# Feed-forwards as block products in Strassen's form, with the sums on GpSimd

## The chip, the cores and the metric

The kernel runs on one core of one Trainium2 chip. Its time is device microseconds (us) of one execution. TensorE (PE in the profile) multiplies, its weight loads have a row of their own (PEld); VectorE (DVE), ScalarE (ACT) and GpSimd (POOL) do the elementwise work; SyncE (SP) issues the transfers. Each engine works through its own queue in order, and queues wait for one another by semaphores.

## The reference

Two layers over 512 tokens of 1024 features, all in float32. Each layer has a feed-forward, a mixer and a second feed-forward, each behind an RMS norm and added to x:

```
swiglu(h) = (silu(h @ w_gate) * (h @ w_up)) @ w_down          # 1024 -> 2816 -> 1024
x = x + 0.5 * swiglu(rmsnorm(x))
x = x + mixer(rmsnorm(x))      # layer 0: short convolution and attention over a memory
                               # layer 1: attention with forget gates, and over the memory
x = x + 0.5 * swiglu(rmsnorm(x))
```

The keys and values of layer 1's attention come from x as it enters that layer, under a norm of its own. A last norm ends it. So there are four feed-forwards, and the change is to them.

## The kernel before

Features lie on the 128 partitions, tokens along the free dimension: x is eight tiles `X[k]` of 128 x 512. Every product of a float32 weight block by a tile is three matmuls (`mm3`, lines 134 to 136): weight and tile are each split in a high and a low float32r part, and high x high, high x low and low x high are added in one PSUM bank of 512 columns. `Normed` splits x times the norm's gain; 1 / rms (`st.row`) is applied behind the product.

`Weights` holds the weights as pieces of up to 1024 columns in the order of use. `load` brings a piece to a raw tile (`wr`, four of them); `begin` splits it: ScalarE copies the high part (`wh`, line 81), VectorE subtracts it from the raw tile (`wl`, line 82), both of them SBUF. `next` hands a piece out and keeps the splits two pieces ahead of TensorE, the loads three.

`ffn` takes the 22 tiles of hidden features in two halves of 11. For a hidden tile TensorE multiplies a gate piece and an up piece by the eight tiles of x (48 matmuls). VectorE scales the gate from PSUM by 1 / rms (L287), ScalarE takes SiLU (L288), VectorE multiplies by the up product (L289), and the result is split (L139, L140). Then eight tiles of the down product take the half's 11 hidden tiles each; L308 scales the bank and L311 adds it to x. GpSimd has no work in a feed-forward. The order on each engine is the program's.

The first 57 us project the memory's keys (matmuls of 256 columns) and values; there, and in the last norm, some sums are on GpSimd (L159, L479, L792).

Of the kernel before, what the change touches and what calls it, by code (L numbers as in the profile page):

```python
# [22 lines left out]
HALVES = [(0, 11), (11, 22)]  # L23
# [12 lines left out]
class Weights:  # L36
    """Pieces of the weights in the order of use: loaded ahead, and split ahead into two float32r
    parts."""

    LOAD, SPLIT = 3, 2  # L40

    def __init__(self, nc, pool):
        self.nc, self.pool = nc, pool
        self.todo, self.raw, self.parts = [], {}, {}
        self.loaded = self.split = self.used = 0

    def add(self, ap, widths=(1024, 1024), step=1024):
        at = 0
        for w in widths:
            self.todo.append((ap[:, at : at + w], step))  # L50
            at += w
        assert at == ap.shape[1]

    def load(self):
        """The next piece, by transfers of step columns."""
        n = self.loaded
        self.loaded += 1
        ap, step = self.todo[n]
        w = ap.shape[1]
        self.raw[n] = self.pool.tile([P, 1024], F32, tag="wr", name=f"wr{n}", bufs=4)  # L60
        for a in range(0, w, step):
            c = slice(a, min(a + step, w))
            self.nc.sync.dma_start(out=self.raw[n][:, c], in_=ap[:, c])
            yield

    def begin(self):
        """The next piece's parts, split by step columns."""
        i = self.split
        self.split += 1
        while self.loaded < min(len(self.todo), i + 1 + self.LOAD):  # L70
            for _ in self.load():
                pass
        ap, step = self.todo[i]
        w, raw = ap.shape[1], self.raw.pop(i)
        hi = self.pool.tile([P, 1024], F32R, tag="wh", name=f"wh{i}", bufs=3)
        lo = self.pool.tile([P, 1024], F32R, tag="wl", name=f"wl{i}", bufs=3)
# [10 lines left out]
    def next(self, ahead=SPLIT):  # L87
        """The next piece's parts; the splits run ahead of it by so many pieces."""
        i = self.used
        self.used += 1  # L90
        while self.split < min(len(self.todo), i + 1 + ahead):
            for _ in self.begin():
                pass
        return self.parts.pop(i)
# [3 lines left out]
def model(ctx: ExitStack, tc: tile.TileContext, A, out):  # L98
# [13 lines left out]
    SLOTS = {"s": 66, "t": 12}  # L112
# [4 lines left out]
    def parts(tag="s"):  # L117
        return slot(tag, F32R), slot(tag, F32R)

# [12 lines left out]
    def mm3(ps, wh, wl, xh, xl, first, last):  # L132
        """One product over 128 rows: high x high, high x low, low x high."""
        nc.tensor.matmul(ps, wh, xh, start=first, stop=False)  # L134
        nc.tensor.matmul(ps, wh, xl, start=False, stop=False)  # L135
        nc.tensor.matmul(ps, wl, xh, start=False, stop=last)  # L136
# [10 lines left out]
    class Stats:  # L147
        """The squares of tiles of 128 features, summed; then 1 / rms by token."""
# [13 lines left out]
        def step1(self, c=None):  # L162
            """The sums over all features, on every partition, and their roots."""
# [14 lines left out]
        def columns(self):  # L178
            """1 / rms of the tokens of each block, by partition."""
# [10 lines left out]
    class Normed:  # L190
        """Tiles of x times a norm's gain, in two parts; 1 / rms is applied behind the product."""
# [14 lines left out]
    def plan_ffn(n):  # L206
        for a, b in HALVES:
            chunks(A["gu"][n, a:b])
            for d in range(KD):
                W.add(A["dn"][n, d][:, a * P : b * P], (6 * P, 5 * P))  # L210
# [17 lines left out]
    plan_ffn(3)  # L228

# [11 lines left out]
    # The tensor engine's clock rises while it works: it does from the first transfers on.  # L241
# [660 lines left out]
```

## Time and profile before

| | |
|---|---|
| time, median of 3 runs | 2038.25 us (2036.89 to 2038.62) |
| the profiled execution, its span | 2038.5 us |
| TensorE busy | 2018.4 us, 99% |
| VectorE busy | 1002.9 us, 49% |
| ScalarE busy | 704.7 us, 35% |
| GpSimd busy | 34.1 us, 2% |
| mean granted TensorE clock | 0.996 |
| HBM | 95 GB/s over the span |

Times in the rows are from the start of the span; the execution's own time is its span, 2038.5 us, a quarter of a microsecond over the median of the runs. A row of a timeline reads: start in us, duration in us, engine, line, operation, written tile <- read tiles, shapes, how many in a row, and in brackets how long the engine sat idle before it and what ended that. A row of a group has busy time and mean duration (ns) after the bar, then the idle time before the group's instructions and what ended it. Durations of matmuls overlap, since they are pipelined: their cost is read from the distance of their starts. `mm` and `aux` are PSUM banks; `s`, `t`, `r`, `wr`, `wh`, `wl` lie in SBUF.

### The profile page before, as it was taken

The page shows a single profiled execution, that of the slowest core. Times are in us where ns is not written, and L with a number is a line of the kernel's source. Part 1 is how long each engine was busy: PE and PEld are TensorE (multiplying, and loading weights), DVE is VectorE, ACT ScalarE, POOL GpSimd, SP SyncE. Part 2 cuts the span into 40 slices and gives each one's busy share as a digit, 9 for nine tenths or more (in the row PEclk, how much of TensorE's full clock was granted, in tenths as well). Part 3 has the DMA queues.
Part 4 walks back from the last instruction along what each step waited for, and adds up shares of the span by engine and source line. Part 5 has one row for each costly group of instructions (what it writes and reads, how often), then busy time and mean ns, then how long its engine had stood idle before and what let it go on. Part 6 is the DMA issues. An engine that isn't in the chain of part 4 may idle for free.

```text
span 2038.5 us, 22628 instructions
## 1 busy us (share of the span) xinstructions
PE 2018.4 (99%) x9175; PEld 1674.7 (82%) x9175; DVE 1002.9 (49%) x1355; ACT 704.7 (35%) x1049; POOL 34.1 (2%) x50
## 2 busy tenths in 40 slices
PE   9999999999999999999999999999999999999997
PEld 8788888888888888888888888888878878888886
DVE  7643434576555443443644343467546664344444
ACT  7422222353224332232432222335335552222233
POOL 2000000000000000000000000000001100000000
PEclk9999999999999999999999999999999999999998
DMA  7322332332222323322322332232221032233222
GB/s 261 105 94 79 117 99 82 99 104 73 98 99 93 100 84 91 118 94 76 120 94 86 91 114 98 80 112 77 80 93 63 32 103 94 84 102 106 98 78 70
DMA packets 62328, 195.73 MB, mean 96 GB/s; under 512 B 7056, under 2 KB 9232, under 8 KB 62224
## 3 DMA queue, kind: packets, MB, share of 16 engines
q1 hardware_dynamic: 62224, 194.30, 30.0%
q8 instruction: 71, 1.16, 0.2%
q14 instruction: 33, 0.27, 0.0%
HBM read 192.17 MB, written 2.10 MB: 95 GB/s over the span
## 4 chain that ended last, share of the span: by engine, by line
PE 98%; DVE 1%; DMA 0%; issue 0%; ACT 0%; SPq 0%; DVEq 0%; ACTq 0%
PE mm L134 32%; PE mm L135 32%; PE mm L136 32%; PE mm L694 0%; PE mm L434 0%; DVE wl L82 0%; DMA s<-in_memT 0%; PE aux L651 0%; DVE s L143 0%; PE mm L666 0%; PE mm L750 0%; PE aux L134 0%; PE aux L136 0%; PE aux L135 0%; PE mm L785 0%
## 5 line engine op out<-in xcount | busy, mean ns | idle before, releaser
L134 PE MATMUL mm<-s,wh 128*128 128x512 f32 (+1 forms) x2763 | 1067.5, 386 | 2.4 <-ACT s L143 1.5
L135 PE MATMUL mm<-s,wh 128*128 128x512 f32 (+1 forms) x2763 | 1066.6, 386 | 0.3
L136 PE MATMUL mm<-s,wl 128*128 128x512 f32 (+1 forms) x2763 | 1066.0, 386 | 0.5 <-DVE wl L82 0.5
L81 ACT ACTIVATE wh<-wr 128x1024 fp32r<-128x1024 f32 (+3 forms) x403 | 390.4, 970 | 1174.1 <-PE mm L135 749.9
L134 PEld LDWEIGHTS mm<-s,wh 128*128 128x128 f32 x2763 | 519.0, 188 | 108.1 <-ACT s L143 2.4
L136 PEld LDWEIGHTS mm<-s,wl 128*128 128x128 f32 x2763 | 518.9, 188 | 105.9 <-DVE wl L82 1.1
L135 PEld LDWEIGHTS mm<-s,wh 128*128 128x128 f32 x2763 | 519.2, 188 | 104.7 <-DVE s L143 0.7
L82 DVE TENSOR_TENSOR wl<-wr,wh 128x1024 fp32r<-128x1024 f32 (+3 forms) x403 | 449.3, 1116 | 190.9 <-ACT wh L81 189.0
L289 DVE TENSOR_TENSOR t<-mm,t 128x512 f32<-128x512 f32 x88 | 60.9, 692 | 289.9 <-PE mm L136 287.0
L287 DVE TENSOR_TENSOR t<-mm,r 128x512 f32<-128x512 f32 x88 | 60.8, 691 | 224.6 <-PE mm L136 224.5
L308 DVE SCALAR_TENSOR_TENSOR t<-mm,r 128x512 f32<-128x512 f32 (+1 forms) x65 | 44.4, 683 | 124.8 <-PE mm L136 124.8
L140 DVE TENSOR_TENSOR s<-t,s 128x512 fp32r<-128x512 f32 (+1 forms) x128 | 86.4, 677 | 2.2 <-ACT s L139 2.0
L139 ACT ACTIVATE s<-t 128x512 fp32r<-128x512 f32 (+1 forms) x128 | 78.6, 616 | 16.5 <-DVE t L547 6.2
L143 DVE SCALAR_TENSOR_TENSOR s<-s,vec,s 128x512 fp32r<-128x512 f32 (+1 forms) x64 | 49.0, 780 | 14.6 <-ACT s L143 14.6
L288 ACT ACTIVATE t<-t 128x512 f32<-128x512 f32 x88 | 54.2, 616 | 3.1 <-DVE t L287 3.1
L143 ACT ACTIVATE s<-s,vec 128x512 fp32r<-128x512 f32 (+1 forms) x64 | 42.9, 688 | 33.3 <-DVE s L311 32.8
L311 DVE TENSOR_TENSOR s<-s,t 128x512 f32<-128x512 f32 (+1 forms) x65 | 45.2, 696 | 0.6
L352 DVE TENSOR_TENSOR s<-s,mm 128x512 f32<-128x512 f32 x32 | 21.8, 686 | 42.3 <-PE mm L136 42.3
L135 PE MATMUL mm<-wl,s 128*128 128x512 f32 x96 | 38.2, 398 | 4.4 <-DVE wl L82 4.4
L155 ACT ACTIVATE t<-s 128x512 f32<-128x512 f32 x59 | 35.9, 617 | 14.1 <-DVE s L311 14.1
L140 DVE TENSOR_TENSOR s<-mm,s 128x512 fp32r<-128x512 f32 (+1 forms) x56 | 34.2, 646 | 12.2 <-ACT s L139 12.1
L686 POOL TENSOR_TENSOR s<-s,s 128x128 fp32r<-128x128 f32 x32 | 13.9, 466 | 1558.8 <-ACT s L685 1558.8
(116 smaller groups left out, 743.7 us busy)
## 6 DMA issues: line engine op xcount, KB each, us to landing
wr<-in_gu SPq DMA_DIRECT2D x176, 512.0 KB, 3.7
wr<-in_dn SPq DMA_DIRECT2D x64, 384.0 KB, 3.1
wr<-in_dn SPq DMA_DIRECT2D x64, 320.0 KB, 2.9
wr<-in_ain SPq DMA_DIRECT2D x28, 512.0 KB, 3.7
wr<-in_wout SPq DMA_DIRECT2D x24, 512.0 KB, 3.7
wr<-in_mkv SPq DMA_DIRECT2D x14, 512.0 KB, 5.2
wr<-in_wq SPq DMA_DIRECT2D x8, 512.0 KB, 3.7
wr<-in_wv SPq DMA_DIRECT2D x8, 512.0 KB, 3.7
```

What stands on the lines that cost most here:

```text
L81: self.nc.scalar.activation(hi[:, c], raw[:, c], AF.Copy),
L82: self.nc.vector.tensor_tensor(out=lo[:, c], in0=raw[:, c], in1=hi[:, c].bitcast(F32), op=ALU.subtract),
L134: nc.tensor.matmul(ps, wh, xh, start=first, stop=False)
L135: nc.tensor.matmul(ps, wh, xl, start=False, stop=False)
L136: nc.tensor.matmul(ps, wl, xh, start=False, stop=last)
L139: nc.scalar.activation(hi, src, AF.Copy)
L140: nc.vector.tensor_tensor(out=lo, in0=src, in1=hi.bitcast(F32), op=ALU.subtract)
L143: return nc.scalar.activation(hi, src, AF.Copy, scale=g), nc.vector.scalar_tensor_tensor(out=lo, in0=src, scalar=g, in1=hi.bitcast(F32), o ...
L287: nc.vector.tensor_tensor(out=t, in0=pg, in1=st.row, op=ALU.mult)
L288: nc.scalar.activation(t, t, AF.Silu)
L289: nc.vector.tensor_tensor(out=t, in0=pu, in1=t, op=ALU.mult)
L311: nc.vector.tensor_tensor(out=y[:, c], in0=new[d][:, c], in1=t[:, c], op=ALU.add)
```

## The change

Each product of the feed-forwards is done by blocks of two by two: weights by halves (A11, A12, A21, A22), tiles of tokens by two blocks of features and two halves of 256 tokens (B11 to B22). Seven products of blocks stand for eight. The sums of the weights' blocks are formed on GpSimd (`Weights.sums`, lines 103 to 106), and those of the tokens' blocks too (`Quad`, lines 274 to 277). For the gate and up products A11 and A12 are the two halves of the contraction of gate, A21 and A22 of up; for the down products the blocks are two tiles of output by even and odd hidden tiles.

A block of weights has four pieces for the splits: A11 with A12, two tiles of sums (`ws`), and A22 alone: seven quarter blocks are split where there were four. Blocks go by twos (`by_two`): each piece of the one is followed by that of the other. `wr`, `ws`, `wh` and `wl` have four tiles each. The products of a block (`products`) go to three banks per item; `gated` and `added` read them in between: ScalarE copies some (L460, L469), VectorE adds others with PSUM as one input (L463, L471, L474, L504). 1 / rms is applied to the gate on VectorE (L465) and to SiLU's result on GpSimd (L467). The hidden tiles are taken in groups of 3, 3, 3 and 2 pairs, each with its part of the down product, which is added to x in place. The very last two tiles of output are done directly by halves of the tokens.

So that SBUF holds this, x of layer 1's start, and the memory's keys and values, are written to DRAM tiles (`keep`) and loaded again where they are used. Names of lines are those of the changed kernel from here on.

```diff
+GROUPS = [(0, 3), (3, 6), (6, 9), (9, 11)]
 class Weights:
-    LOAD, SPLIT = 3, 2
+    LOAD, SUMS, SPLIT = 8, 5, 2
...
+    def sums(self):
+        item, q = self.units[self.summed]
+        self.summed += 1
+        if q is None or "s" in item:
+            return
+        self.load_to(self.summed)
+        w, (r0, r1) = item["w"], item["r"]
+        a11, a12, a22, a21 = r0[:, :w], r0[:, w : 2 * w], r1[:, :w], r1[:, w : 2 * w]
+        item["s"] = sa, sb = [self.tile("ws") for _ in range(2)]
+        tt = self.nc.gpsimd.tensor_tensor
+        tt(out=sa[:, :w], in0=a21, in1=a22, op=ALU.add)
+        tt(out=sa[:, w : 2 * w], in0=sa[:, :w], in1=a11, op=ALU.subtract)
+        tt(out=sb[:, :w], in0=a12, in1=sa[:, w : 2 * w], op=ALU.subtract)
+        tt(out=sb[:, w : 2 * w], in0=a11, in1=a21, op=ALU.subtract)
...
+    class Quad:
+        def __init__(self, b1, b2, whole=False):
+            ts = slot("t"), slot("t")
+            b11, b12, b21, b22 = b1[:, :H], b1[:, H:], b2[:, :H], b2[:, H:]
+            t1, t2, t3, t4 = ts[0][:, :H], ts[0][:, H:], ts[1][:, :H], ts[1][:, H:]
+            tt = nc.gpsimd.tensor_tensor
+            tt(out=t1, in0=b12, in1=b11, op=ALU.subtract)
+            tt(out=t2, in0=b22, in1=t1, op=ALU.subtract)
+            tt(out=t4, in0=b21, in1=t2, op=ALU.subtract)
+            tt(out=t3, in0=b22, in1=b12, op=ALU.subtract)
+            self.two(b11, "B11")
+            self.four(b2, "B21", "B22")
+            self.four(ts[0], "T1", "T2")
+            self.four(ts[1], "T3", "T4")
...
+    UNITS = [("B11", "B21"), ("T1", "T2"), ("B22", "T3"), ("T4",)]
+    def products(items, quads, early=()):
...
+        def product(b, ps, w, half, n, ks):
+            for k in ks:
+                c = slice((half * nk + k) * P, (half * nk + k + 1) * P)
+                begins = n in ("B11", "B21", "T1")
+                first = begins and k == (early or late)[0]
+                mm3(ps[:, :H], w[0][:, c], w[1][:, c], *quads[k].of[n], first, k == late[-1], not begins)
...
-                nc.vector.tensor_tensor(out=t, in0=pg, in1=st.row, op=ALU.mult)
-                nc.scalar.activation(t, t, AF.Silu)
-                nc.vector.tensor_tensor(out=t, in0=pu, in1=t, op=ALU.mult)
+                if said in ("x1", "x2"):
+                    nc.scalar.activation(g[:, :H] if said == "x1" else g[:, H:], ps, AF.Copy)
+                elif said in ("y", "z2"):
+                    o = g[:, :H] if said == "y" else g[:, H:]
+                    nc.vector.tensor_tensor(out=o, in0=ps, in1=o, op=ALU.add)
+                    if said == "z2":
+                        nc.vector.tensor_tensor(out=g, in0=g, in1=st.row, op=ALU.mult)
+                        nc.scalar.activation(g, g, AF.Silu)
+                        nc.gpsimd.tensor_tensor(out=g, in0=g, in1=st.row, op=ALU.mult)
+                elif said == "z1":
+                    nc.scalar.activation(h[:, H:], ps, AF.Copy)
+                elif said == "x3":
+                    nc.vector.tensor_tensor(out=h[:, H:], in0=ps, in1=h[:, H:], op=ALU.add)
+                    nc.vector.tensor_tensor(out=h[:, H:], in0=h[:, H:], in1=g[:, H:], op=ALU.mult)
+                else:
+                    nc.vector.tensor_tensor(out=h[:, :H], in0=ps, in1=g[:, :H], op=ALU.mult)
...
-    X0, st2 = X, st
-    X, st, (nd,) = ffn(2, X, nd, st2, [V_MIX + 8], fresh=True)
+    X0 = [keep(x) for x in X]
+    X, st, (nd,) = ffn(2, X, quads.quads, st2, [lambda: Normed(V_MIX + 8)])
```

How the work of the engines moves is seen from the order of their instructions. GpSimd had nothing between the first and the last of these rows of the kernel before, from the last sum of the first norm to the attention of layer 1, with three feed-forwards in between:

```order
L159 TENSOR_TENSOR t_462<-t_462,t_674 128x512
L686 TENSOR_TENSOR s_10954<-s_10647,s_10953 128x128
```

In the changed kernel it has this for each pair of hidden tiles in the middle of the first feed-forward (`ws` are the sums of weights, `r` is 1 / rms, the last four rows are a quad's sums):

```order
L103 TENSOR_TENSOR ws_2428<-wr_2326 128x512
L106 TENSOR_TENSOR ws_2429<-wr_2325,wr_2326 128x512
L104 TENSOR_TENSOR ws_2428<-ws_2428,wr_2325 128x512
L105 TENSOR_TENSOR ws_2429<-wr_2325,ws_2428 128x512
L467 TENSOR_TENSOR t_2317<-t_2317,r_878 128x512
L103 TENSOR_TENSOR ws_2465<-wr_2362 128x512
L106 TENSOR_TENSOR ws_2466<-wr_2361,wr_2362 128x512
L104 TENSOR_TENSOR ws_2465<-ws_2465,wr_2361 128x512
L105 TENSOR_TENSOR ws_2466<-wr_2361,ws_2465 128x512
L467 TENSOR_TENSOR t_2319<-t_2319,r_878 128x512
L274 TENSOR_TENSOR t_2569<-t_2318 128x256
L275 TENSOR_TENSOR t_2569<-t_2320,t_2569 128x256
```

Two more quad sums (L277, L276) end the pair's fourteen instructions. On VectorE a hidden tile had five instructions before, in the same feed-forward:

```order
L287 TENSOR_TENSOR t_849<-mm_793,r_756 128x512
L82 TENSOR_TENSOR wl_821<-wr_703,wh_820 128x1024
L289 TENSOR_TENSOR t_849<-mm_824,t_849 128x512
L82 TENSOR_TENSOR wl_860<-wr_734,wh_859 128x1024
L140 TENSOR_TENSOR s_854<-t_849,s_853 128x512
```

Now a pair of hidden tiles has 23, of which these follow one another in the middle of the pair whose GpSimd rows stand above:

```order
L130 TENSOR_TENSOR wl_2462<-wr_2103,wh_2461 128x512
L130 TENSOR_TENSOR wl_2502<-wr_2133,wh_2501 128x512
L463 TENSOR_TENSOR t_2317<-mm_2397,t_2317 128x256
L465 TENSOR_TENSOR t_2317<-t_2317,r_878 128x512
L471 TENSOR_TENSOR t_2318<-mm_2329,t_2318 128x256
L472 TENSOR_TENSOR t_2318<-t_2318,t_2317 128x256
L130 TENSOR_TENSOR wl_2536<-wr_2325,wh_2535 128x1024
L463 TENSOR_TENSOR t_2319<-mm_2434,t_2319 128x256
L471 TENSOR_TENSOR t_2320<-mm_2365,t_2320 128x256
L465 TENSOR_TENSOR t_2319<-t_2319,r_878 128x512
L130 TENSOR_TENSOR wl_2553<-wr_2361,wh_2552 128x1024
L474 TENSOR_TENSOR t_2318<-mm_2329,t_2317 128x256
```

The weight splits moved closer together, with reads of PSUM (`mm`) between them; L472 needs what GpSimd's L467 wrote, and L467 needs L465 by way of SiLU.

More of the change, by code (lines that the diff above doesn't have):

```diff
@@ L326, in ffn, with pairs @@
+        def pairs(p):
+            pair(p)
+            if not any(p == b for _, b in GROUPS) and p != GROUPS[-1][1] - 1:
+                combine(p)
+        order_ffn(pairs, down)
         return new, nst, nxt
@@ L717, in model @@
     )
-    st, (nd,) = op.finish()
+    st, (quads,) = op.finish()
     class Last:
```

373 lines of the change are left out of this document (264 added, 109 removed).

## The prediction

> **What bounds the kernel now.** I read the page first: engines, the chain that ended last, the DMA queue's share of the 16 engines, and the DMA issues.
>
> ```profile
> PE 2018.4 (99%) x9175; PEld 1674.7 (82%) x9175; DVE 1002.9 (49%) x1355; ACT 704.7 (35%) x1049; POOL 34.1 (2%) x50
> PE 98%; DVE 1%; DMA 0%; issue 0%; ACT 0%; SPq 0%; DVEq 0%; ACTq 0%
> q1 hardware_dynamic: 62224, 194.30, 30.0%
> wr<-in_gu SPq DMA_DIRECT2D x176, 512.0 KB, 3.7
> ```
>
> The chain is TensorE for 98% of the span, VectorE has half its time free, GpSimd nearly all. A busy PE row doesn't say what one matmul costs, so I took the pitch from the timeline of VectorE in the first feed-forward: L287 reads one gate tile of each hidden tile.
>
> ```profile
> 100.16 0.69 DVE L287 TENSOR_TENSOR t<-mm,r 128x512 f32<-128x512 f32 x1 [2.70 <-PE mm L136]
> ...
> 111.04 0.69 DVE L287 TENSOR_TENSOR t<-mm,r 128x512 f32<-128x512 f32 x1 [2.70 <-PE mm L136]
> ```
>
> 10.88 us for a hidden tile of 48 matmuls is 0.2267 us for one of 512 columns. A feed-forward has 22 x 48 + 8 x 66 = 1584 of them, 359 us; four take 1436 us, and all the rest of the 2038.5 us span is 602 us. (The sums are made against this span, which lies 0.25 us over the median of the runs, 2038.25 us.) So any gain must come from matmul time, and a loss from anything that starves it.
>
> **Matmuls, removed and added.** Seven products for eight leave 7/8 of the columns, but each matmul is now 256 wide, so there are 2772 in a feed-forward. That form runs already where the memory's keys are projected; first and last row of 59 in a row on TensorE's timeline:
>
> ```profile
> 37.77 0.28 PE L135 MATMUL mm<-s,wh 128*128 128x256 f32 x1
> ...
> 44.73 0.28 PE L136 MATMUL mm<-s,wl 128*128 128x256 f32 x1
> ```
>
> 58 steps in 6.96 us: 0.120 us each, 6% over half of 0.2267. So 2772 x 0.120 = 333 us for 359: 26 us a feed-forward, 105 us in all, is the gain if TensorE stays the bound. Per pair of hidden tiles (168 matmuls) that is 20.2 us for 21.8.
>
> **VectorE and GpSimd, each for itself.** The prices are means of the groups by shape (L82 splits weights on VectorE, L81 on ScalarE; L140 splits activations; L308 reads PSUM), and single rows for 256 columns and for GpSimd:
>
> ```profile
> L82 DVE TENSOR_TENSOR wl<-wr,wh 128x1024 fp32r<-128x1024 f32 x270 | 332.3, 1232 | 94.5 <-ACT wh L81 93.0 <-PE mm L136 1.0
> L140 DVE TENSOR_TENSOR s<-t,s 128x512 fp32r<-128x512 f32 x120 | 82.1, 685 | 2.2 <-ACT s L139 2.0
> L82 DVE TENSOR_TENSOR wl<-wr,wh 128x768 fp32r<-128x768 f32 x64 | 61.3, 958 | 0.3
> L81 ACT ACTIVATE wh<-wr 128x1024 fp32r<-128x1024 f32 x270 | 286.2, 1061 | 842.8 <-PE mm L135 465.6 <-issue 363.9 <-PE mm L136 11.5
> ...
> 44.98 0.41 DVE L140 TENSOR_TENSOR s<-t,s 128x256 fp32r<-128x256 f32 x1
> 2025.33 0.42 DVE L308 SCALAR_TENSOR_TENSOR t<-mm,r 128x256 f32<-128x256 f32 x1 [2.12 <-PE mm L136]
> ...
> 21.05 0.74 POOL L479 TENSOR_TENSOR t<-t 128x256 f32<-128x256 f32 x1
> 2024.49 2.50 POOL L792 TENSOR_TENSOR t<-s,t 128x512 f32<-128x512 f32 x2 [395.83 <-ACT t L787]
> ```
>
> Per pair VectorE now has six weight splits of 1024 and two of 512 (six + two x 0.69: 7.4 + 1.4), the quad's splits (2 x 0.69 + 0.41 = 1.8), L465 twice and L472 twice (2 x 0.69 + 2 x 0.41 = 2.2): 12.8 us whose two inputs both lie in SBUF. L463, L471 and L474 add eight reads of PSUM at 0.42: 3.4 us. Together 16.2 us, under the 20.2 of TensorE. GpSimd has eight weight sums and two L467 of 512, and four sums of 256. At 1.25 (2.50 for two) and 0.74 that is 10 x 1.25 + 4 x 0.74 = 15.5 us, under 20.2 as well. ScalarE splits the same pieces in a little less time. Looked at one by one, nothing but TensorE is full. That reading would give a gain.
>
> **VectorE and GpSimd together.** GpSimd works beside VectorE only in the first 57 us and the last 15. These timeline rows of both engines decide the forecast:
>
> ```profile
> 18.82 2.15 POOL L159 TENSOR_TENSOR t<-t,t 128x512 f32<-128x512 f32 x1
> 45.66 1.56 POOL L159 TENSOR_TENSOR t<-t,t 128x512 f32<-128x512 f32 x1 [2.61 <-ACT t L155]
> 48.12 6.16 POOL L159 TENSOR_TENSOR t<-t,t 128x512 f32<-128x512 f32 x4 [0.91 <-ACT t L155]
> 54.55 1.41 POOL L159 TENSOR_TENSOR t<-t,t 128x512 f32<-128x512 f32 x1 [0.27 <-ACT t L155]
> ...
> 18.01 1.81 DVE L82 TENSOR_TENSOR wl<-wr,wh 128x1024 fp32r<-128x1024 f32 x1 [1.80 <-ACT wh L81]
> 46.50 1.80 DVE L82 TENSOR_TENSOR wl<-wr,wh 128x1024 fp32r<-128x1024 f32 x1
> 48.22 1.52 DVE L140 TENSOR_TENSOR s<-t,s 128x256 fp32r<-128x256 f32 x1
> 49.66 5.17 DVE L143 SCALAR_TENSOR_TENSOR s<-s,vec,s 128x512 fp32r<-128x512 f32 x3
> 54.76 2.28 DVE L82 TENSOR_TENSOR wl<-wr,wh 128x1024 fp32r<-128x1024 f32 x1
> 56.97 0.74 DVE L143 SCALAR_TENSOR_TENSOR s<-s,vec,s 128x512 fp32r<-128x512 f32 x1
> 2025.79 1.48 DVE L311 TENSOR_TENSOR s<-s,t 128x256 f32<-128x256 f32 x1
> ```
>
> The split at 46.50 starts while the GpSimd sum of 45.66 runs until 47.22; it takes 1.80 for 1.23, late by 0.57, about what was left of that sum. L140 at 48.22 takes 1.52 for 0.41, L311 at 2025.79 takes 1.48 for 0.42: each waits for the GpSimd operation in front of it. The other way round, the sum of 18.82 takes 2.15 since the split of 18.01 to 19.82 is in its way. L308 at 2025.33 has one input in PSUM and takes 0.42 in the middle of a GpSimd operation: unhurt. So VectorE instructions with two SBUF inputs and GpSimd's sums take turns; PSUM readers don't mind.
>
> The Trainium skill says this as a rule: by its page "SBUF — State Buffer", section "Who interferes with whom", a VectorE instruction with two SBUF inputs and a GpSimd instruction that reads SBUF share one read path, and the second to come waits for the whole of the first. The rows above agree; what the rule would give to the letter is a rival below.
>
> *What a turn costs.* With both engines supplied, VectorE's three L143 take 5.17 us and GpSimd's four sums 6.16: 1.72 and 1.54 a turn, mean 1.63 for 512 columns on either side. The split of 54.76 ends at 57.04, 1.08 after the sum of 54.55 ended, so 1024 columns hold the path for 1.08 us, 512 for 0.54; that leaves 1.09 us to a GpSimd sum of 512 (estimates from these rows). Less than the 1.25 and 0.69 of the single instructions, for a start overlaps the other's end.
>
> *Per pair*: GpSimd 10 x 1.09 + 4 x 0.55 = 13.1; VectorE 6 x 1.08 + 2 x 0.54 (weights), 1.35 (quad), 1.62 (L465, L472) = 10.5. Sum 23.6 us, where TensorE needs 20.2 and the old pair took 21.8. That is the lower bound of a pair. The upper one, no overlap at all, is 16.2 + 15.5 = 31.7. The PSUM reads can run while GpSimd has its turn, so the lower end is nearer; but the engines work in order, GpSimd waits for SiLU between sums, and tiles for sums and raw weights are four each. I take 25.5.
>
> *Down products*, per step of two items over three pairs (126 matmuls, 15.1 us; the same work was 72 x 0.2267 = 16.3): GpSimd 8 sums of 384, some 0.82 each: 6.5; VectorE 6 splits of 768 at 0.81 and 2 of 384 at 0.41: 5.7. Path 12.2, under 15.1. VectorE alone is 6 x 0.96 + 2 x 0.55 + 14 x 0.42 (L504) = 12.7, and 19.2 if every sum delays it in full. Near the row of TensorE: 16.5. The groups are 3, 3, 3 and 2 pairs, so 7.33 such steps: 121 us (bounds 111 and 141), for 120 before: no gain.
>
> *Seams*: at each feed-forward's end four quads of x add 16 sums of 256 (8.8 us of the path) and their splits (5.4), part of it under matmuls: 10 us each, bounds 0 and 20. In the first 57 us of the program the same engines already stop TensorE:
>
> ```profile
> 25.00 0.50 PE L135 MATMUL mm<-wl,s 128*128 128x512 f32 x1 [0.77 <-DVE wl L82]
> 25.34 0.40 PE L136 MATMUL mm<-wh,s 128*128 128x512 f32 x1
> ...
> 57.10 0.50 PE L135 MATMUL mm<-wl,s 128*128 128x512 f32 x1 [3.67 <-DVE wl L82]
> 58.62 0.63 PE L134 MATMUL mm<-wh,s 128*128 128x512 f32 x1
> 59.05 0.63 PE L135 MATMUL mm<-wl,s 128*128 128x512 f32 x1
> ```
>
> Weight sums and quads come on top there: 10 us, bounds 0 and 20. After the stop of 3.67 us at 57.10 matmuls come 0.43 apart, half speed, for some 3 us; after the pause of 0.77 us at 25.00, nearer to what a turn costs, they do not (0.34, then 0.24), so I add nothing for the clock.
>
> *Tiles kept in DRAM*: X, keys and values go out and come back on SP's queue, 48 transfers of 256 KB beside DMA engines that are 30% busy; they are asked for many matmuls ahead and cost nothing. If that cover fails, the first head's keys are late once per mixer, some 4 us each.
>
> *Sum*: 11 x 25.5 + 121 + 10 = 412 us a feed-forward for 359; four: 1646; with 602 and 10 for the start: 2258. I predict **2260 us**, 11% slower. Bounds from the terms: 11 x 23.6 + 111 = 371, so 2086; and 11 x 31.7 + 141 + 20 = 510, so 2660 (the start at 0 and 20).
>
> **Rivals.**
>
> *TensorE stays the bound (faster).* If the turns cost little in a steady stream, because GpSimd's sums fall into times when VectorE reads PSUM or waits, a feed-forward is 333 + 10, four 1372, the whole 1974 us. For it: each engine alone has a fifth of its time to spare. Against it: the path needs 23.6 us in 20.2. It decides once a pair falls under 20.7 us (11 x 20.7 + 131 = 359), that is if holds are an eighth shorter than I read them, and no turn is lost. Chance 0.13.
>
> *Turns of whole instructions (slower still).* If each side holds the path for its full duration, a pair is 12.8 + 15.5 = 28.3, a feed-forward 11 x 28.3 + 131 = 442, the whole 2380 us. For it: L311 lost 1.06, nearly a whole sum. Against it: 1.63 a turn is less than 1.25 + 0.69. The rule of the Trainium skill's SBUF page, taken to the letter, is this case. Chance 0.12.
>
> *The ring of weight tiles, not the path.* Four raw tiles hold one pair's two blocks. The second half of a block is free when its last piece is split; then come the load (3.7), eight sums or products of GpSimd in order (8 x 1.25) and the splits on ScalarE and VectorE (1.06 + 1.23): 16 us, against the 144 matmuls, 17.3 us, from that piece's split to the need of the next. That just fits; at 1.63 a sum it is 3 late, 23.2 a pair, and with down steps and seams as above 4 x 386 + 612 = 2157 us. GpSimd would then sit waiting for DMA. Chance 0.08.
>
> **How the numbers follow.** The forecast (VectorE and GpSimd in turns bind the gate-up products) has 0.67, with its own range 2100 to 2370. Faster is the first rival, 0.13. About 0.2%, 4 us, is what a measurement of this kernel can tell from no change; a total that close would be a coincidence of the ends, 0.02. Slower: 0.85. The range 2060 to 2450 holds the forecast, the ring and most of the third case, and leaves out the first.
>
> **What would show it.** In the changed profile: the split of 1024 columns (L130) at a mean of 1.8 us or more for 1.23 while the PSUM readers (L463, L504) stay at 0.42; GpSimd's 512 sums (L103 to L106) at 1.5 or more; in a feed-forward's middle VectorE over 90% busy, TensorE's matmuls in bursts with gaps released by wl, and 25 us from one pair's L467 to the next; about 16.5 for two down items. VectorE and GpSimd should replace TensorE in the chain. I am wrong if L130 stays near 1.23, or if TensorE has no gaps within the gate-up products. A pair at 28 would speak for whole turns, GpSimd idle behind DMA for the ring, rows of matmuls at 0.24 apart for a clock that I left out.

## The result: 16% slower, and the profile after

The changed kernel takes 2370.1 us (median of four runs, 2368.91 to 2373.64) beside 2037.57 us of the kernel before on the same chip (2036.55 to 2038.62): a ratio of 1.1634, with a 95% interval of 1.1617 to 1.165. The prediction was 2260 us, range 2060 to 2450. The page of the profiled run, engines, chain and TensorE's granted clock by slices:

```profile
PE 2064.5 (87%) x13908; PEld 1917.3 (81%) x13908; DVE 1834.8 (77%) x2444; ACT 1061.2 (45%) x1769; POOL 1343.7 (57%) x982
PEclk9899999999999999999889999999999989999998
PE 46%; DVE 19%; POOL 18%; DMA 7%; issue 5%; ACT 4%; SPq 0%; DVEq 0%; POOLq 0%; ACTq 0%
```

TensorE held 98% of the chain; now it has less than half, and VectorE, GpSimd and the transfers share the rest. No engine is full. What each instruction costs stands in the groups by shape (VectorE first, then GpSimd):

```profile
L130 DVE TENSOR_TENSOR wl<-ws,wh 128x1024 fp32r<-128x1024 f32 x176 | 279.0, 1585 | 39.2 <-ACT wh L129 39.2
L130 DVE TENSOR_TENSOR wl<-wr,wh 128x1024 fp32r<-128x1024 f32 x183 | 266.5, 1458 | 42.0 <-ACT wh L129 41.8
L204 DVE TENSOR_TENSOR s<-t,s 128x512 fp32r<-128x512 f32 x212 | 264.1, 1261 | 16.0 <-ACT s L203 14.7
L504 DVE SCALAR_TENSOR_TENSOR s<-mm,s 128x256 f32<-128x256 f32 x441 | 175.9, 415 | 20.8 <-PE mm L200 16.5
L472 DVE TENSOR_TENSOR t<-t,t 128x256 f32<-128x256 f32 x88 | 73.1, 831 | 182.7 <-POOL t L467 182.7
L463 DVE TENSOR_TENSOR t<-mm,t 128x256 f32<-128x256 f32 x176 | 72.2, 412 | 9.1 <-PE mm L200 9.1
...
L104 POOL TENSOR_TENSOR ws<-ws,wr 128x512 f32<-128x512 f32 x88 | 164.4, 1868 | 0.3
L103 POOL TENSOR_TENSOR ws<-wr 128x512 f32<-128x512 f32 x88 | 139.9, 1590 | 166.6 <-DMA wr<-in_gu 145.2 <-DVE s L504 14.9 <-DVE wl L130 6.4
```

VectorE's instructions with two SBUF inputs are longer on average (the 1024-column split 1.46 to 1.59 us for 1.23, the 512-column split of activations 1.26 for 0.69), the readers of PSUM (L504, L463) are at their 0.41 to 0.42, and GpSimd's 512-column weight sums (L103 to L106) average 1.5 to 1.9 for 1.25. Two waits are new: VectorE's L472 for the product L467 that stands in GpSimd's queue (182.7 us), and GpSimd's first sum for its raw tile (145.2).

Where the time lies in the program shows in ScalarE's timeline at L466 (SiLU, two a pair of hidden tiles): the first of the second feed-forward, two middle pairs, a pair with two down steps, and the first of the third feed-forward. Then the same two ends in the kernel before (its L288).

```profile
767.24 0.63 ACT L466 ACTIVATE t<-t 128x512 f32<-128x512 f32 x1
...
820.36 0.63 ACT L466 ACTIVATE t<-t 128x512 f32<-128x512 f32 x1 [6.96 <-DVE t L465]
846.64 0.63 ACT L466 ACTIVATE t<-t 128x512 f32<-128x512 f32 x1 [5.87 <-DVE t L465]
907.85 0.63 ACT L466 ACTIVATE t<-t 128x512 f32<-128x512 f32 x1 [3.16 <-DVE t L465]
...
1217.99 0.63 ACT L466 ACTIVATE t<-t 128x512 f32<-128x512 f32 x1
```

```profile
668.24 0.63 ACT L288 ACTIVATE t<-t 128x512 f32<-128x512 f32 x1 [0.59 <-DVE t L287]
...
1027.79 0.63 ACT L288 ACTIVATE t<-t 128x512 f32<-128x512 f32 x1 [0.59 <-DVE t L287]
```

From one feed-forward to the next it is 450.8 us for 359.6. In that stretch the six pairs that follow a pair directly are 26.1 to 27.9 us apart, mean 26.8. The three that have two down steps between them are 59.6 apart on average, 16.4 a step. Eleven pairs (294.8) and 7.33 steps (120.3) leave **35.7 us for the seam** between the two feed-forwards.

Busy time by stretch: the columns are the stretch and its length, then for PE, PEld, DVE, ACT and POOL the busy us (and instructions), the granted clock, the DMA share and GB/s. A middle pair, and two stretches of the seam:

```profile
820.40:846.70 26.30, 21.02 (x171) 20.39 (x170) 21.05 (x25) 12.06 (x21) 20.05 (x14) 1.00 0.23 67
...
1160.00:1180.00 20.00, 9.86 (x49) 9.30 (x50) 17.45 (x25) 10.18 (x18) 13.49 (x12) 0.57 0.29 80
1180.00:1200.00 20.00, 13.31 (x70) 11.25 (x68) 17.57 (x18) 10.67 (x19) 16.97 (x13) 0.74 0.35 118
```

In this pair TensorE, VectorE and GpSimd are each busy 76 to 80%, no more. Over the six pairs VectorE is busy 22.2 of 26.8 us on average (80 to 90%), at a granted clock of 0.91 to 1.00. In the two stretches of the seam TensorE has a third to a half of its time free, and its granted clock is 0.57 and 0.74.

### The profile page after: what moved, and what is told of

The parts are those of the page before. It is cut to its first block, busy times and chain, and to the rows that moved or that the text cites. A ratio compares the mean times of both kernels' runs of the same rounds, so it can differ in the third digit from the quotient of the medians.

```text
span 2368.9 us, 35874 instructions
## 1 busy us (share of the span) xinstructions
PE 2064.5 (87%) x13908; PEld 1917.3 (81%) x13908; DVE 1834.8 (77%) x2444; ACT 1061.2 (45%) x1769; POOL 1343.7 (57%) x982
## 4 chain that ended last, share of the span: by engine, by line
PE 46%; DVE 19%; POOL 18%; DMA 7%; issue 5%; ACT 4%; SPq 0%; DVEq 0%; POOLq 0%; ACTq 0%
PE mm L198 15%; PE mm L200 15%; PE mm L199 15%; DVE wl L130 8%; DVE s L204 5%; DMA wr<-in_gu 5%; POOL ws L104 4%; POOL ws L106 3%; POOL ws L103 3%; POOL t L467 3%; POOL ws L105 2%; DMA wr<-in_dn 2%; ACT wh L129 2%; DVE t L472 2%; DVE s L504 1%
## 5 line engine op out<-in xcount | busy, mean ns | idle before, releaser
L198 PE MATMUL mm<-s,wh 128*128 128x256 f32 (+1 forms) x4338 | 1342.6, 311 | 164.2 <-DVE t L471 86.7
L200 PE MATMUL mm<-s,wl 128*128 128x256 f32 (+1 forms) x4338 | 1331.3, 308 | 80.5 <-DVE wl L130 80.2
L199 PE MATMUL mm<-s,wh 128*128 128x256 f32 (+1 forms) x4338 | 1329.4, 307 | 17.1 <-DVE s L204 16.4
L198 PEld LDWEIGHTS mm<-s,wh 128*128 128x128 f32 x4338 | 869.2, 201 | 215.4 <-DVE t L471 96.1
L200 PEld LDWEIGHTS mm<-s,wl 128*128 128x128 f32 x4338 | 868.5, 201 | 116.6 <-DVE wl L130 93.0
L199 PEld LDWEIGHTS mm<-s,wh 128*128 128x128 f32 x4338 | 871.3, 201 | 44.6 <-DVE s L204 20.8
L129 ACT ACTIVATE wh<-wr 128x1024 fp32r<-128x1024 f32 (+4 forms) x402 | 332.0, 827 | 460.4 <-PE mm L199 344.6
L130 DVE TENSOR_TENSOR wl<-wr,wh 128x1024 fp32r<-128x1024 f32 (+4 forms) x402 | 465.1, 1164 | 75.3 <-ACT wh L129 74.9
L130 DVE TENSOR_TENSOR wl<-ws,wh 128x1024 fp32r<-128x1024 f32 (+2 forms) x302 | 415.6, 1376 | 64.3 <-ACT wh L129 64.3
L129 ACT ACTIVATE wh<-ws 128x1024 fp32r<-128x1024 f32 (+2 forms) x302 | 282.5, 941 | 188.1 <-POOL ws L104 98.1
L103 POOL TENSOR_TENSOR ws<-wr 128x512 f32<-128x512 f32 (+2 forms) x151 | 218.2, 1445 | 253.2 <-DMA wr<-in_gu 145.2
L204 DVE TENSOR_TENSOR s<-t,s 128x512 fp32r<-128x512 f32 (+1 forms) x282 | 316.7, 1139 | 16.9 <-ACT s L203 15.6
L104 POOL TENSOR_TENSOR ws<-ws,wr 128x512 f32<-128x512 f32 (+2 forms) x151 | 256.8, 1701 | 1.6
L106 POOL TENSOR_TENSOR ws<-wr,wr 128x512 f32<-128x512 f32 (+2 forms) x151 | 253.6, 1680 | 0.0
L467 POOL TENSOR_TENSOR t<-t,r 128x512 f32<-128x512 f32 x88 | 121.6, 1382 | 175.3 <-ACT t L466 175.3
L472 DVE TENSOR_TENSOR t<-t,t 128x256 f32<-128x256 f32 x88 | 73.1, 831 | 182.7 <-POOL t L467 182.7
L504 DVE SCALAR_TENSOR_TENSOR s<-mm,s 128x256 f32<-128x256 f32 x441 | 175.9, 415 | 20.8 <-PE mm L200 16.5
L466 ACT ACTIVATE t<-t 128x512 f32<-128x512 f32 x88 | 55.5, 631 | 293.7 <-DVE t L465 293.7
```

The costliest lines, as they stand in the source:

```text
L103: tt(out=sa[:, :w], in0=a21, in1=a22, op=ALU.add)
L104: tt(out=sa[:, w : 2 * w], in0=sa[:, :w], in1=a11, op=ALU.subtract)
L106: tt(out=sb[:, w : 2 * w], in0=a11, in1=a21, op=ALU.subtract)
L129: self.nc.scalar.activation(hi[:, c], raw[:, c], AF.Copy),
L130: self.nc.vector.tensor_tensor(out=lo[:, c], in0=raw[:, c], in1=hi[:, c].bitcast(F32), op=ALU.subtract),
L198: nc.tensor.matmul(ps, wh, xh, start=first, stop=False, skip_group_check=more)
```

## The experiments

The theory on record: VectorE instructions with two SBUF inputs and GpSimd's sums take turns, and that makes the pairs long. The rivals: GpSimd's queue is simply full or in the wrong order; the ring of raw tiles holds the sums back; the halved clock. Ratios are to the kernel before, on the same chip.

### The turns alone

No model: stages of 24 instructions on VectorE, GpSimd or both, on constant tiles; the output isn't computed.

```
for n in (256, 512, 1024): 24 x vector a - b           # both in SBUF
24 x vector psum - b
for n in (256, 512): 24 x gpsimd a + b;  24 x gpsimd memset 512
together: vector 512 + gpsimd 512; vector 1024 + gpsimd 512; vector 256 + gpsimd 256;
          96 x vector psum 256 + gpsimd 512; vector 1024 + 48 x gpsimd memset 512
```

> This kernel leaves the whole model out: it runs stages of 24 VectorE subtractions and 24 GpSimd sums, each engine alone and then side by side, and writes zeros. Turns (the forecast's theory): alone VectorE takes 0.69 for 512 columns and 1.23 for 1024, GpSimd 1.25 for 512. Side by side 512 by 512 goes at 1.6 us a turn, 39 us for 24 pairs; 1024 by 512 at 2.2 us, 52 us; VectorE with one input in PSUM (256 columns, four times as many) keeps 0.42 beside GpSimd's 1.25. A rival without a shared path: 512 by 512 takes 30 us, 1024 by 512 takes 30 us. Whole-instruction turns (the second rival of the prediction): 1.9 a turn, 46 us, and 2.5, 59 us. The stage with GpSimd memsets tells whether an operation that only writes takes turns too; no theory of mine says so.

VectorE's timeline (start, us of all 24 or 96), then GpSimd's:

```profile
23.29 14.53 DVE L40 TENSOR_TENSOR vo<-va,vb 128x512 f32<-128x512 f32 x24
38.45 27.33 DVE L40 TENSOR_TENSOR vo<-va,vb 128x1024 f32<-128x1024 f32 x24
...
134.26 39.01 DVE L40 TENSOR_TENSOR vo<-va,vb 128x512 f32<-128x512 f32 x24
174.96 51.81 DVE L40 TENSOR_TENSOR vo<-va,vb 128x1024 f32<-128x1024 f32 x24
...
249.85 31.88 DVE L43 TENSOR_TENSOR vo<-ps,vb 128x256 f32<-128x256 f32 x96
282.37 27.32 DVE L40 TENSOR_TENSOR vo<-va,vb 128x1024 f32<-128x1024 f32 x24
```

```profile
91.70 29.29 POOL L46 TENSOR_TENSOR po<-pa,pb 128x512 f32<-128x512 f32 x24
121.39 11.25 POOL L49 MEMSET po<- 128x512 f32 x24
133.06 39.67 POOL L46 TENSOR_TENSOR po<-pa,pb 128x512 f32<-128x512 f32 x24
...
248.65 29.39 POOL L46 TENSOR_TENSOR po<-pa,pb 128x512 f32<-128x512 f32 x24
282.19 22.45 POOL L49 MEMSET po<- 128x512 f32 x48
```

Alone, 512 columns take VectorE 0.605 us and a GpSimd sum 1.22; together 1.64 a turn (24 turns in 39.01 us by VectorE's row, 39.67 by GpSimd's), 2.16 with 1024 on VectorE's side. Readers of PSUM beside the same sums lose nothing (0.332 us each, 0.335 alone), and neither does the 1024-column subtraction beside GpSimd's fills, which read nothing. The Trainium skill ("SBUF — State Buffer", "Who interferes with whom") says the same of readers of PSUM and of GpSimd instructions that only write, and the rows agree. With the rule of the same page that the second side waits for the whole of the first they don't agree: a turn is 1.64 us, not 1.22 + 0.605 = 1.83.

### Without the weight sums

```diff
-        tt(out=sa[:, :w], in0=a21, in1=a22, op=ALU.add)
-        ... three more
+        item["s"] = item["r"]        # the raw halves are split in their place
```

> The changed kernel without GpSimd's sums of weights; the pieces of sums are split from the raw weights instead, so that splits, matmuls and all else stay in number and size. Turns: a pair's path falls from 23.6 to 14.9 us, TensorE's 20.2 binds, a feed-forward is 11 x 20.6 + 111 + 15 = 353, the whole some 2020 us. Queue (VectorE's L472 waits for GpSimd's L467, which stands behind sums that wait for weights): the same, since the sums are gone. If block products of 256 columns, their PSUM reads or the clock cost more than I reckoned, it stays over 2100.

The sums are left out, so the products no longer make up the model's output. 2016.9 us, 0.9887 (0.9872 to 0.9902), as expected. A middle pair:

```profile
711.80:732.00 20.20, 20.20 (x170) 20.20 (x169) 17.06 (x25) 12.22 (x20) 7.71 (x6) 1.00 0.28 87
```

The 353 us that hang on the weight sums are gone, and TensorE binds the pair, at just the 20.2 us of the prediction. From one feed-forward to the next it is 358.1 us, though, where 333 was TensorE's sum: 11 x 20.2 and 7.33 x 15.35 leave 23 us of seam even here.

### The same sums on VectorE

```diff
-        tt = self.nc.gpsimd.tensor_tensor
+        tt = self.nc.vector.tensor_tensor
```

and the same for the quads' sums (L273) and L467.

> The changed kernel with every GpSimd operation of the feed-forwards (sums of weights, sums of tokens, L467) on VectorE, GpSimd idle there. Turns: a pair is VectorE's own 16.2 + 8 x 0.69 + 4 x 0.41 + 2 x 0.69 = 24.7 with no turn to wait for, 11 x 25 + 7.33 x 17.1 + 20 = 420 a feed-forward, 2290 us: faster than the changed kernel's 2370 although VectorE gets half as much work again. If GpSimd truly relieves VectorE and the loss is elsewhere (queues, buffers, clock), 8.5 us a pair more on VectorE make it slower: 2500 or more.

2115.2 us, 1.0371 (1.0356 to 1.0387), far under both expectations.

```profile
742.20:763.80 21.60, 20.41 (x167) 19.91 (x166) 21.60 (x39) 12.43 (x21) 0.00 (x0) 1.00 0.27 78
```

VectorE does 14 instructions more and needs 21.60 us, against 21.05 in the same pair of the changed kernel. Over the six pairs of the second feed-forward it is busy 21.8 us on average here and 22.2 in the changed kernel: GpSimd's help saves VectorE nothing. My 2290 had added durations; back to back, instructions overlap (0.605 us for 512 columns above, 0.69 by its duration).

### GpSimd's products ahead of its sums

```diff
-    LOAD, SUMS, SPLIT = 8, 5, 2
+    LOAD, SUMS, SPLIT = 8, 2, 2
+            self.tc.keep_in_program_order(self.nc.gpsimd.tensor_tensor(**k))     # each weight sum
+            tc.keep_in_program_order(nc.gpsimd.tensor_tensor(out=g, in0=g, in1=st.row, op=ALU.mult))
```

> The changed kernel with GpSimd's order pinned: both L467 of a pair go ahead of the next pair's weight sums, so that L472 on VectorE no longer waits behind sums that wait for weights. Number and size of all operations are unchanged. Queue: the 5.2 us a pair that VectorE stands at L472 go, 27.2 becomes 22, 2140 us. Turns alone: the path's 23.6 a pair stays, so at best 24, 2230 us, and less if other waits take the place. If the order doesn't matter: 2370.

2447.1 us, 1.2009 (1.1989 to 1.2029), above all that was expected. ScalarE's wait for the sums, and VectorE's at L472 for L467 (L475 and L470 in this kernel; us in total, times, longest):

```profile
ACT wh L131 <- POOL ws L103: 542.1, 175, 6.0
...
DVE t L475 <- POOL t L470: 89.0, 80, 1.7
```

VectorE's wait at L472 was halved, 89 us for 182.7, and the weight sums came late instead: ScalarE waits 542.1 us for L103; in the changed kernel its largest wait for a weight sum, L104, is 98.1 us in all. So L467's place in the queue is not by itself the loss. The run doesn't exclude an order in between, since the sums were also asked for later, two pieces ahead in place of five.

### GpSimd as busy, without reading

```diff
+        for s in (sa, sb):
+            tt(out=s[:, :8], in0=a21[:, :8], in1=a11[:, :8], op=ALU.subtract)
+            for _ in range(3):
+                self.nc.gpsimd.memset(s[:, 8 : 2 * w], 0.5)
```

in place of a block's four sums.

> The four weight sums of a block are left out; in their place GpSimd fills the same two tiles with a constant, three fills over each tile, behind one eight-column subtraction of the block's two halves that keeps the wait for both transfers. A fill of 512 columns took 0.469 us alone, so a block of 1024-column tiles holds GpSimd some 5.6 us, against the 6.2 us of its four sums in the changed kernel (mean 1.55 us each); the queue, its order and its waits for the weights stay, and only the turns on the shared path go, since a fill took none in the first run. Turns theory: VectorE is back at 14.2 us a pair, TensorE binds at 20.2, and the kernel lands near the one without sums, 2015 to 2060 us, with the 1024-column subtraction back near 1.2 us. Rival (GpSimd's occupied queue and its waits for the transfers are what the pairs wait for): the pairs stay near 27 us and the time at 2300 us or above.

2052.0 us, 1.0064 (1.0047 to 1.008), in the range of the turns theory; the sums are missing from this output too.

```profile
723.20:743.90 20.70, 20.41 (x170) 20.20 (x169) 16.88 (x24) 12.02 (x21) 18.43 (x24) 1.00 0.24 71
```

GpSimd is busy for 18.43 us of the pair (20.05 in the changed kernel) in the same queue with the same waits for the transfers, and VectorE is back from 21.05 to 16.88 us. The occupied queue is not quite free: one early pair of each feed-forward takes 23.0 to 25.7 us, the others that follow a pair directly 20.2 to 21.5, and the whole is 35 us above the run without the sums. But 318 of the 333 us that the change cost are gone with the reads of the weight sums. This run settles that the turns are the root.

### The weight sums alone on GpSimd

The quads' sums and L467 go to VectorE, the weight sums stay.

> The quads' sums and the multiplication by the norm's row move from GpSimd to VectorE; the weight sums stay on GpSimd, so nothing that VectorE waits for in a pair stands behind them in GpSimd's queue any more. Turns theory, as a sum: VectorE alone has 14.2 us a pair without any sums (the 21.6 us pair of the run with all sums on VectorE, less 8 x 0.605, 4 x 0.338 and 2 x 0.605); each weight sum beside it adds 1.64 - 0.605 = 1.03 us (8.3 us), and the moved work 2.6 us: 25.1 us a pair. The same sum for the changed kernel is 14.2 + 10 x 1.03 + 4 x 0.52 = 26.6, so 44 pairs give back 66 us, the seams perhaps 15 more: 2270 to 2310 us. Rival (the wait behind GpSimd's queue is the loss): with the wait gone the pairs fall to 20 to 22 us, and the time to 2150 us or below.

2280.1 us, 1.1183 (1.1166 to 1.12), where the turns were expected to bring it.

```profile
795.70:820.30 24.60, 21.21 (x162) 20.80 (x161) 24.16 (x31) 12.26 (x21) 12.33 (x8) 0.93 0.23 71
```

Here VectorE is full, 24.16 of 24.6 us (98%), and its sum of 25.1 us, each sum of GpSimd lengthening it by 1.03, fits: the six pairs of the second feed-forward average 25.2. The same sum gave 26.6 for the changed kernel's pair and seemed to fit as well, but there VectorE is busy only 21.05 of 26.3: that agreement was chance. About five microseconds of that pair are waits.

### TensorE kept busier

```diff
+                        nc.tensor.matmul(ps[:, :H], w[0][:, c], nought, start=False, stop=False, ...)
```

twice in every gate and up product, ahead of its last block; `nought` is a tile of zeros.

> The changed kernel with two more 256-column matmuls against a tile of zeros behind every gate and up product: 28 a pair, 28 x 0.120 = 3.4 us of TensorE, no work for VectorE or GpSimd, the output unchanged. It asks whether TensorE's halved clock costs the pairs anything (0.944 on average in the changed kernel, half clock in 268 us of its span). VectorE theory: the sum 14.2 + 10 x 1.03 + 4 x 0.52 = 26.6 us makes the pair with no term for the clock, and TensorE's 20.2 + 3.4 = 23.6 us stay below it: 2360 to 2390 us, with fewer stretches at half clock. Rival one (the halved clock is on the path): with TensorE busier the clock is granted more, and the time falls below 2345 us. Rival two (TensorE's products and VectorE's work follow each other in a pair instead of running side by side): 44 x 3.4 us are added, 2500 us or more.

2404.2 us, 1.1799 (1.178 to 1.1819): 34 us more, between the theories. The mean clock rose from 0.944 to 0.958 and no gain shows. The run can't tell a small gain by the clock from the cost of the added matmuls; but the middle pair quoted above takes its 26.3 us at a granted clock of 1.00, so the clock is not what makes it long. Over the 44 pairs 0.8 of the added 3.4 us a pair show. That would fit TensorE's work and VectorE's following one another in part, in a cycle of waits; it isn't shown.

### Six raw tiles

```diff
-    LOAD, SUMS, SPLIT = 8, 5, 2
+    LOAD, SUMS, SPLIT = 12, 5, 2
-            item["raw"] = self.tile("wr")
+            item["raw"] = self.tile("wr", bufs=6)       # and three tiles of wh and wl for four
```

> The changed kernel with six tiles for weights as they are loaded, in place of four, and transfers issued 12 pieces ahead in place of eight; the room comes from the split weights, three tiles of each part in place of four, as the kernel before has them. VectorE theory: GpSimd's 253 us of idle time before its first sum, put down to the transfers, is slack, since a pair's 26.6 us are VectorE's: 2350 to 2385 us. Rival (the ring of raw tiles holds the sums back, and with them the pairs): the waits for the transfers go and the time falls to 2300 us or below. A third outcome, later than 2385 us, would say that the fourth tile of the split parts does more than the ring.

2303.1 us, 1.1307 (1.129 to 1.1324): 67 us faster, close to the rival's 2300, so the ring is part of the cause. The same pair as above (the six average 26.0 us, for 26.8):

```profile
805.10:830.20 25.10, 21.73 (x170) 21.56 (x170) 21.84 (x24) 12.58 (x21) 21.58 (x15) 0.93 0.21 59
```

And GpSimd's waits before a block's first sum, in the changed kernel and then here (us in total, times, longest):

```profile
POOL ws L103 <- DMA wr<-in_gu: 145.2, 53, 4.2
...
POOL ws L103 <- DMA wr<-in_gu: 221.7, 2, 220.9
POOL ws L103 <- DVE wl L130: 130.3, 39, 6.1
```

The 53 waits of the changed kernel for raw tiles of gate and up are gone but for one long one, 220.9 us, before a feed-forward begins. In their place GpSimd waits 39 times for a split of VectorE, 130.3 us in all: the wait has moved and is not gone. VectorE and GpSimd are each at 86 to 87% of a pair of 25.1 us.

### Both of the last two changes

The weight sums alone on GpSimd, and six raw tiles.

> The kernel with the weight sums alone on GpSimd (2280 us) together with the six raw tiles that took the changed kernel from 2370 to 2303 us. In a middle pair of the changed kernel VectorE is busy 21.05 of 26.3 us, of the one with the weight sums alone on GpSimd 24.16 of 24.6. If the ring only fills time in which VectorE waits, it has nothing to fill here: 2270 to 2285 us, pairs still near 25. Rival (the ring holds back GpSimd's sums whoever is full): the same 60 to 70 us again, 2210 to 2220 us. If VectorE is the bound here, its time a pair (14.2 + 8 x 1.03 + 2.6 = 25.1) should stand whatever the ring does.

2255.7 us, 1.1066 (1.1047 to 1.1084): 24 us under the run with four tiles, neither nothing nor the 67 of the other.

```profile
790.90:814.60 23.70, 20.53 (x158) 20.30 (x158) 22.76 (x32) 12.38 (x20) 11.91 (x9) 0.93 0.22 65
```

The pair is shorter by 0.9 us although VectorE had been at 98%: its busy time fell too, from 24.16 to 22.76. Of the 22 VectorE instructions of a pair that read no PSUM, 10.2 run while GpSimd runs one of its own in the run with four tiles, and 8.1 with six (counted on the timelines, mean of 24 pairs). So the number of turns is no constant of the work.

### The down products alone, and a version faster than both

Gate and up go back to whole products, with both norm parts of x in place of its quads; the down products stay in seven; all sums are VectorE's.

```diff
-        order_ffn(lambda p: by_two([A["gu"][n, 2 * p], A["gu"][n, 2 * p + 1]]), down)
+        order_ffn(lambda p: chunks(A["gu"][n, 2 * p : 2 * p + 2]), down)
-        ... gated(j), products(its, quads, ...)
+        ks = (0, 1, 4, 5, 2, 3, 6, 7)        # the order of the eight tiles of x
+        pg = project(quads, ks=ks)
+        pu = project(quads, mid=st.step1 if j == 0 else None, ks=ks)
```

> Gate and up go back to whole products (the former projection, with both norm parts of x in place of its quads), the down products stay in Strassen's form, and all sums are VectorE's. Per pair TensorE has its former 21.8 us and VectorE about 12; per step of two down items TensorE 15.1 and VectorE 14.1, against 16.3 of TensorE before. No quads of x stand between two feed-forwards. If each stage costs what its slowest engine has, a feed-forward saves 7.33 x 1.2 = 9 us, four of them 35, less some us where a group's quads are late: 2000 to 2025 us, ratio 0.98 to 0.995. Rival (the down groups pay for their quads as the seams do, 5 us or more a group): 2040 to 2090 us.

2045.4 us, 1.0033 (1.0022 to 1.0044), above the expected 2000 to 2025 and in the rival's range, but the loss isn't where the rival had it. The SiLUs of two pairs with two down steps between them are 52.1 us apart, so a step is 15.2 us, TensorE's, as expected; but the end of a feed-forward isn't:

```profile
992.50:1013.00 20.50, 14.91 (x100) 13.92 (x98) 19.26 (x44) 10.12 (x19) 0.00 (x0) 0.85 0.41 128
```

In the last group, two pairs instead of three, VectorE is busy 19.26 of 20.50 us and TensorE 14.91. A piece of the short group feeds TensorE for 12 matmuls of 0.12 us, and VectorE has its split, its sums, and the next norm's parts of x as well. So I gave the last group whole down products too, and put its gate and up products ahead of the third group's down products (the tiles of x are taken in their plain order again):

```diff
+            for d in range(KD):
+                w, ps = W.next(), bank()
+                for f, x in enumerate(hid):
+                    mm3(ps, *block(w, f), *x, f == 0, f == len(hid) - 1)
```

> As the run with the down products alone, but the last group of two pairs has whole down products too, eight of 12 matmuls of 512 columns each, and its two pairs of gate and up stand ahead of the third group's down products. Slowest engine by stage: a last-group step of two Strassen items on two pairs had 10.1 us of TensorE but some 11.6 of VectorE, with the next norm's parts and squares behind it (another 8 x 1.4 us); whole, its eight tiles have 21.8 us of TensorE against 8 x 2.6 = 21 of VectorE. If the seams of that run (10 to 12 us each of three, and about as much at the end) are this overload, three groups of 1.2 x 2 us are saved per feed-forward, 7 us, four of them 29, and the seams are nearly gone: 2005 to 2025 us, ratio 0.984 to 0.993, faster than both kernels. Rival (the seam is the wait for the next norm's parts whatever the form of the last group): 2040 to 2050 us as before.

**2012.5 us**, 0.988 (0.9864 to 0.9897), as expected: 1.2% faster than the kernel before. ScalarE's first SiLU of the second and of the third feed-forward, and the engines on the page:

```profile
660.73 0.63 ACT L464 ACTIVATE t<-t 128x512 f32<-128x512 f32 x1 [0.59 <-DVE t L463]
...
1013.62 0.63 ACT L464 ACTIVATE t<-t 128x512 f32<-128x512 f32 x1 [0.59 <-DVE t L463]
```

```profile
PE 1990.4 (99%) x10470; PEld 1713.6 (85%) x10470; DVE 1343.8 (67%) x2185; ACT 802.6 (40%) x1217; POOL 37.2 (2%) x50
```

352.9 us a feed-forward for 359.6: 6.7 saved of the 7.2 that three groups of two steps at 1.2 us can give. There is no seam.

## Why the prediction was right, and where its numbers were off

**The direction and its cause hold.** "VectorE and GpSimd in turns bind the gate-up products": without the reads of GpSimd's weight sums, with GpSimd nearly as busy, the loss falls from 333 to 14 us.

**The price of a turn holds.** 1.63 us was read from seven instructions at the program's start, as the mean of 1.72 and 1.54; 24 measured turns gave 1.64. That it is so close is in part luck. The PSUM readers stayed at 0.41 to 0.42. The tell for GpSimd's 512-column sums, 1.5 us or more, holds. The split of 1024 columns came to 1.46 to 1.59 us, not the 1.8 named, since not every instruction meets a sum: of the 16 VectorE instructions of a pair that read no PSUM, 11.8 run while GpSimd runs one of its own (mean of 24 pairs). The prediction says that GpSimd works beside VectorE only at the two ends of the kernel before; it also has 32 operations of 128 columns in the attention of layer 1. Nothing in the sum rests on that.

**A pair, 25.5 us, is 26.8**: 14 us of the error in a feed-forward. The size is near; the working behind it is not all right. The quad's splits are three of 512 columns and one of 256, not two and one, so a pair has 24 VectorE instructions, not 23, and by the prediction's own prices the path is 24.1 us, not 23.6, and VectorE alone 16.9, not 16.2. "VectorE over 90% busy" failed, it is 80 to 90%. TensorE's gaps come with the weight splits, as named (80.2 us end with one, before L200), but just as much with L471, a reader of PSUM (86.7 us, before L198). The path was taken as the bound with 1.9 us of loss on top, but the loss is larger and in part has a name. The rival "ring of weight tiles" had 0.08, and its sign, GpSimd idle behind transfers, is there (145.2 us). It works beside the turns, not in their place: six raw tiles take 67 us away. Its own sum was off: 1.63 us a sum makes the chain 19.0 us, 1.7 over the 17.3, not 3, and its time about 2100. As I read it, turns lengthen sums and splits, and with four raw tiles a late split delays a load, and that the next sum. How the remaining waits of a pair divide between this ring, L467's place in the queue and the rest of the cycle stays open.

**A down step, 16.5 us, is 16.4.** TensorE's 15.1 us nearly decide: without the weight sums a step is 15.35.

**The ends, 10 us each with bounds 0 and 20, are the term that was mis-sized.** From SiLU to SiLU (each feed-forward's first), in us:

| from | to | before | after | more |
|---|---|---|---|---|
| the start | the first feed-forward | 75.1 | 98.9 | 23.8 |
| the first | the second, a mixer between | 593.1 | 668.3 | 75.2 |
| the second | the third | 359.6 | 450.8 | 91.2 |
| the third | the fourth, a mixer between | 650.0 | 731.6 | 81.6 |
| the fourth | the end | 360.7 | 419.3 | 58.6 |

Eleven pairs and the down steps, 415.1 us, account for some 56 of each feed-forward's excess. Beyond them the four lose 20, 36, 26 and 3 us, in two cases with whatever the mixer between them loses, and the start 24: 108 us where the sum had 50. The pairs are 44 x 1.3 = 57 us above theirs. So the 112 us by which the kernel is later than the sum lie by halves in the pairs and in the ends, and the seam between the second and the third feed-forward, 35.7 us, is the worst of the ends.

I priced only the path that VectorE and GpSimd share. Of the 35.7 us 23 are there without any weight sum, when TensorE binds the pairs, and 26 with nothing on GpSimd at all (383.1 us, less 11 pairs of 21.8 and 7.33 steps of 15.9), so most of them come with the form and not with the turns. The last group has two pairs, its pieces are short for TensorE and full price for VectorE, and the quads of x must be finished behind the last sums into x. The run with whole gate and up products still had 10 to 15 us a seam, with the last group whole none. Another 12 come with the weight sums on GpSimd.

**The clock.** "I add nothing for the clock" was read from a pause of 0.77 us. For the quoted pair that stands, its clock was 1.00; other pairs had 0.91 and more, and what that costs is open. In the seam TensorE stands still for 6.82 us before 1166 us, and the clock was 0.57 and 0.74 in the stretches quoted. From 1136 to 1218 us it was halved for 41 us, and TensorE was busy in 24 of them, so 12 us, half of these, is the most that the clock can have cost there (an estimate; the share itself was not measured).

**The start, 10 us**: the first SiLU comes at 98.9 us, in the run without weight sums at 88.1 and in the kernel before at 75.1. So the weight sums cost 11 us there. The other 13 are not the weight sums'; some 7.5 of them only move to the feed-forward's end, since SiLU now stands behind 108 matmuls of 0.120 us where it had 24 of 0.2267 before it (an estimate).

**The rival nearest in time, whole turns, 2380 us, was right by accident.** It wanted a pair of 28.3 us and turns of 1.25 + 0.69 = 1.94 us; measured are 26.8 and 1.64. What it had too much in the pairs the ends made up.

**TensorE stays the bound** needed the pair under 20.7 us. It gets there only where the weight sums don't read on GpSimd (20.2 us without them; 20.2 to 21.5 in most pairs with fills in their place), and even then the whole takes 2017 us or more, not 1974, since the ends remain.

## What to carry to other kernels

Before work is given to an idle engine, price it beside what the neighbour does at the same time: here GpSimd's sums cost VectorE as much time as doing all of them itself. A scheme that saves matmuls pays its sums and its short pieces at the ends of stages too, so price each stage, its ends above all, by its slowest engine, and use the form only where that engine has the room: the down products in full groups gain 1.2%, everything at once loses 16%.

## What the runs showed of the hardware that I had not expected

- GpSimd's fills of 512 columns at 0.469 us take no turn at all: 48 of them ran beside 24 subtractions of 1024 columns in 22.45 us, and those took 27.32 us for 27.33 alone.
- How much VectorE loses to the same GpSimd sums depends on how many of its instructions meet one: with four raw tiles 10.2 of 22 a pair and 24.16 us busy in the pair quoted, with six 8.1 and 22.76.
- TensorE at half to two thirds of its time busy (9.86 and 13.31 of 20 us) had a granted clock of 0.57 and 0.74; in the pair quoted above, at 80% busy, 1.00, and in the other pairs of that feed-forward 0.91 to 1.00.
